# Splitting two scaling steps of a chunked scan between VectorE and ScalarE, and pinning its transposes behind output products

## The chip, the cores and the metric

The kernel runs on one core of a Trainium2 chip. Its engines work side by side, each through its own instructions in order: TensorE (PE in the profile; PEld is its loading of weights), VectorE (DVE), ScalarE (ACT), GpSimd (POOL) and SyncE (SP), whose queue issues the DMA transfers. The metric is device time in microseconds, the median of several runs. All arrays are float32.

## What is computed

One layer over 1024 latent tokens of width 1024, with 256 context tokens ahead. The mixer makes one projection u, splits its columns among a scan, a Fourier mixing and a pooling, and joins the three through w_out. Then comes a feed-forward part with a convolution. Cut to the mixer:

```python
def ssd_chunked(X, dA, B, C, init_state):     # chunks of 128 tokens
    ...
    y_diag = jnp.einsum("bclhn,bcshn,bhcls,bcshp->bclhp", C, B, Lmat, X)
    ...
    y_off = jnp.einsum("bclhn,bchpn,bhcl->bclhp", C, states, jnp.exp(A_cs))
    return (y_diag + y_off).reshape(b, L, h, p), final_state

def ssd_gate_norm(y, xs, z, d_skip, norm_w):
    bsz, L = z.shape[:2]
    y = (y + xs.astype(jnp.float32) * d_skip.astype(jnp.float32)[:, None]).reshape(bsz, L, SSD_WIDTH)
    y = (y * jax.nn.silu(z.astype(jnp.float32))).reshape(bsz, L, SSD_GROUPS, SSD_WIDTH // SSD_GROUPS)
    y = (y * lax.rsqrt(jnp.mean(y * y, -1, keepdims=True) + EPS)).reshape(bsz, L, SSD_WIDTH)
    return (y * norm_w).astype(z.dtype)

def token_mixer(...):
    xs, bm, cm, dt, dA = ssd_prep(u, ...)
    y, s_f, s_b = ssd_bidir(xs, bm, cm, dt, dA, init_f, init_b)
    y_ssd = ssd_gate_norm(y, xs, u[..., OFF_Z:OFF_XBC], d_skip, norm_w)
    y_fnet = fourier_mix(u[..., OFF_FNET:OFF_POOL], fnet_w)
    y_pool = pool_mix(u[..., OFF_POOL:N_IN], pool_w, pool_scale)
    return jnp.concatenate([y_ssd, y_fnet, y_pool], axis=-1) @ w_out, s_f, s_b
```

## The kernel before, in words

The scan has 8 heads of 64 columns in 2 groups, and runs over 8 chunks of 128 tokens in both directions (d = 0, 1). The change touches the stretch from about 240 to 400 us, between the input projection and the second pair of output tiles.

**States.** state_step(n, d) makes one step of the recurrence: xw on POOL (L685), two products on PE into pst (L710), the old state times its decay on DVE (128x512, L712), plus pst (L715), and a store to s_scratch on SP (L717). The steps are issued between the products of the Fourier and pooling projections. four_weights loads cf (two DMAs, L732 and L733) and multiplies it on PE into pPQ (L738).

**Chunk outputs.** chunk_load brings M (the local products), S (the states) and z (the gate) of a chunk. chunk_y starts y on POOL (L900), makes the products po with the states (two, one for each group) and pd with M on PE (L908, L912), scales po by the decay ecs into t1 on DVE (two instructions of 128x512, one for each group, L914), adds pd (L918) and the two directions of t1 (L920), multiplies by z (L921), and sums the squares on ScalarE (L924 to L928: Square with a sum, Ln, Exp). chunk_norm refines the inverse root by a newton step on 128x2 numbers (sv at L933, then L146, L147, L148 and L150) and multiplies y by it (L935). chunk_out transposes y on PE into pyt (L940), and ScalarE writes yT (L944). Y(i) issues the norm of the chunk before, the y of chunk order[i], and the transposes of the chunk before; the order is 4, 5, 6, 7, 3, 2, 1, 0. There is one buffer of t1 and two each of y, M, S and z.

**Pooling.** pool_mix subtracts the inputs from the pooled sums and mends the edges on DVE (L860, L863, L864), then multiplies on PE into ppool (L871).

**Output products.** out_tiles((7, 6), todo) sums the output tiles pout7 and pout6 over eight slices k of 128 of the 1024 joined columns, in the order KO = 0, 1, 2, 3, 4, 6, 5, 7 (L1010). Each float32 factor is held as a high and a low part (L218 and L219: woh and wol of the weights, yh and yl of the inputs), and three of the four products are summed. wo_prep(i) loads slice KO[i] of w_out into one of two raw buffers (wor, L974), multiplies it by the gate's row g1b (L975; g1b is loaded in wo_prep(0), L971), and splits it: the multiplication on POOL for odd i and on DVE for even i, the low part on the other of the two. fp_split and y_split do the same for the Fourier, pooled and scanned inputs. todo[i] is issued ahead of the products of the i-th slice:

```python
    todo = {
        0: [lambda: fp_split(0, 2, 1), lambda: wo_prep(5), lambda: pool_mix(1, p1), lambda: wo_prep(6), lambda: fp_split(3), lambda: wo_prep(7)],
        1: [Y(5)],
        3: [Y(6)],
        4: [Y(7)],
        7: [Y(8)],
    }
    out_tiles((7, 6), todo)
```

The code gives the instructions in program order; a scheduler then sets each engine's order, so work that is ready early can move ahead of its place in the code.

## Time and profile before

| | us |
|---|---|
| median of 3 runs (1203.28 to 1203.91) | 1203.84 |
| the profiled execution | 1204.77 |
| its span | 1202.9 |
| PE busy in it | 1129.9 (94%) |
| DVE busy | 984.6 (82%) |
| POOL busy | 609.5 (51%) |
| ACT busy | 461.1 (38%) |

The granted clock of PE is 0.981 of its full speed over the whole span. The busy shares are means over stages that differ, so the stretch of the change is read by itself. In the rows below, times are microseconds from the start of the span unless marked ns. A timeline row gives start, duration, engine, line, operation, out<-in, shape and count, and in brackets the idle time of the engine just before with what ended it. Chunk and buffer numbers are left out of names: y is the y of any chunk.

### The profile page before, as it was taken

The page shows a single profiled execution, that of the slowest core. Times are in us where ns is not written, and L with a number is a line of the kernel's source. Part 1 is how long each engine was busy: PE and PEld are TensorE (multiplying, and loading weights), DVE is VectorE, ACT ScalarE, POOL GpSimd, SP SyncE. Part 2 cuts the span into 40 slices and gives each one's busy share as a digit, 9 for nine tenths or more (in the row PEclk, how much of TensorE's full clock was granted, in tenths as well). Part 3 has the DMA queues.
Part 4 walks back from the last instruction along what each step waited for, and adds up shares of the span by engine and source line. Part 5 has one row for each costly group of instructions (what it writes and reads, how often), then busy time and mean ns, then how long its engine had stood idle before and what let it go on. Part 6 is the DMA issues. An engine that isn't in the chain of part 4 may idle for free.

```text
span 1202.9 us, 15202 instructions
## 1 busy us (share of the span) xinstructions
PE 1129.9 (94%) x5328; PEld 918.1 (76%) x5328; DVE 984.6 (82%) x1395; ACT 461.1 (38%) x790; POOL 609.5 (51%) x482
## 2 busy tenths in 40 slices
PE   4999999989878999899999999999999999999986
PEld 1698887777756787788888787888888888888864
DVE  4788787688899789799999968787777877777966
ACT  1273566721344232433232343333333334343553
POOL 0010122244254025664556477767676767676756
PEclk9999999999999999899999999999999999999988
DMA  9849465567524404223555346665556555555513
GB/s 309 283 163 324 128 213 167 170 195 221 189 89 166 148 35 141 97 88 108 172 166 176 118 154 219 192 199 175 182 183 190 193 192 190 188 184 184 197 40 140
DMA packets 151875, 206.48 MB, mean 172 GB/s; under 512 B 12253, under 2 KB 89067, under 8 KB 151799
## 3 DMA queue, kind: packets, MB, share of 16 engines
q1 hardware_dynamic: 151799, 205.51, 52.7%
q8 instruction: 42, 0.69, 0.2%
q14 instruction: 34, 0.28, 0.1%
HBM read 148.76 MB, written 56.71 MB: 171 GB/s over the span
## 4 chain that ended last, share of the span: by engine, by line
PE 69%; DVE 16%; DMA 6%; issue 3%; ACT 3%; POOL 2%; SPq 0%; DVEq 0%; ACTq 0%; POOLq 0%
PE pu L1353 22%; PE pdn L1187 16%; PE pu L1527 9%; PE pout L1010 4%; PE px L445 4%; PE pz L344 4%; PE pl L1584 3%; PE p L1353 3%; DMA bc<-cs_scratch 2%; DVE cv L1234 1%; PE pu L1245 1%; POOL cv L1224 1%; DMA xr<-in_x_dram 1%; DMA zb_r<-in_w_in_dram 1%; PE pm L298 1%
## 5 line engine op out<-in xcount | busy, mean ns | idle before, releaser
L1234 DVE SCALAR_TENSOR_TENSOR cv<-pu,ffc,cv 128x945 f32<-128x945 f32 (+6 forms) x362 | 425.6, 1180 | 74.1 <-ACT cv L1212 64.3
L1187 PE MATMUL pdn<-wd,gh 128*128 128x512 f32 x576 | 180.7, 395 | 0.3 <-DVE xt L1190 0.3
L1187 PEld LDWEIGHTS pdn<-wd,gh 128*128 128x128 f32 x576 | 108.2, 188 | 25.8 <-DVE xt L1190 1.0
L1187 PE MATMUL pdn<-wd,gl 128*128 128x512 f32 x288 | 113.6, 394 | 0.0
L1190 DVE TENSOR_TENSOR xt<-xt,pdn 128x512 f32<-128x512 f32 x128 | 87.4, 683 | 28.8 <-PE pdn L1187 24.4
L219 POOL TENSOR_TENSOR wul<-wur,wuh 128x1024 fp32r<-128x1024 f32 x29 | 72.3, 2495 | 39.3 <-ACT wuh L218 30.7
L1455 POOL TENSOR_TENSOR wdr<-wdr,g2b 128x512 f32<-128x512 f32 x44 | 57.4, 1309 | 54.7 <-DMA wdr<-in_ffn_w_down_dram 53.1
L219 POOL TENSOR_TENSOR S<-wur,S 128x384 fp32r<-128x384 f32 (+2 forms) x75 | 62.6, 861 | 36.8 <-ACT S L218 24.4
L1481 POOL TENSOR_TENSOR cv<-cv,cv 128x512 f32<-128x512 f32 x44 | 57.9, 1336 | 27.7 <-ACT cv L1480 27.7
L1212 ACT ACTIVATE cv<-pu,ffc 128x1024 f32<-128x1024 f32 (+3 forms) x46 | 53.4, 1164 | 43.5 <-PE pu L1353 21.5
L1353 PE MATMUL pu<-T,S 128*128 128x512 f32 x270 | 67.5, 393 | 0.4 <-POOL S L219 0.4
L644 POOL TENSOR_TENSOR bc<-bc,ncs 128x256 f32<-128x256 f32 x32 | 25.7, 807 | 76.4 <-DMA bc<-cs_scratch 62.1
L1187 PEld LDWEIGHTS pdn<-wd,gl 128*128 128x128 f32 x288 | 54.1, 188 | 12.8
L1480 ACT ACTIVATE cv<-cv 128x512 f32<-128x512 f32 x44 | 25.5, 625 | 90.9 <-DVE cv L1234 90.9
L1353 PEld LDWEIGHTS pu<-T,S 128*128 128x128 f32 x270 | 50.5, 188 | 12.8 <-POOL S L219 0.8
L1353 PE MATMUL pu<-h2h,wuh 128*128 128x512 f32 x150 | 59.1, 394 | 0.0
L206 POOL TENSOR_TENSOR h2l<-h2t,h2h 128x512 fp32r<-128x512 f32 x14 | 20.5, 1475 | 75.9 <-DVE h2h L205 75.9
L1353 PE MATMUL pu<-h2h,wul 128*128 128x512 f32 x150 | 59.0, 393 | 0.0
L1353 PE MATMUL pu<-h2l,wuh 128*128 128x512 f32 x150 | 58.5, 390 | 0.0
L219 POOL TENSOR_TENSOR gl<-cv,gh 128x512 fp32r<-128x512 f32 x44 | 56.7, 1309 | 1.5 <-PE pl L1584 0.7
L219 POOL TENSOR_TENSOR wd<-wdr,wd 128x512 fp32r<-128x512 f32 x42 | 53.8, 1303 | 4.7 <-ACT wd L218 4.6
L1527 PE MATMUL pu<-h2h,wuh 128*128 128x512 f32 x176 | 55.3, 395 | 0.0
(407 smaller groups left out, 2939.6 us busy)
## 6 DMA issues: line engine op xcount, KB each, us to landing
xt<-x_scratch SPq DMA_DIRECT2D x144, 256.0 KB
x_scratch<-xt SPq DMA_DIRECT2D x144, 256.0 KB
wur<-in_ffn_w_up_dram SPq DMA_DIRECT2D x44, 512.0 KB
wad<-in_w_ada_dram SPq DMA_DIRECT2D x32, 512.0 KB
wdr<-in_ffn_w_down_dram SPq DMA_DIRECT2D x44, 256.0 KB
wa<-in_w_ada_dram SPq DMA_DIRECT2D x32, 256.0 KB
bc<-cs_scratch SPq DMA_DIRECT2D x32, 256.0 KB
xr<-in_x_dram SPq DMA_DIRECT2D x8, 512.0 KB
```

The lines of the kernel that those rows point to most:

```text
L219: return (eng or G).tensor_tensor(lo, raw, hi.bitcast(F32), op=ALU.subtract)
L344: TE.matmul(pt[:, j * 512 : j * 512 + ZW], a, b[:, k % 4, :], start=first and i == 0, stop=last and i == 2)
L445: TE.matmul(pt[:, q * 512 : q * 512 + 512], a[:, k, :], b[q][:, k, :], start=k == 0 and i == 0, stop=k == KD - 1 and i == 2)
L1010: TE.matmul(pt[:, nb * 512 : nb * 512 + 512], u, v[:, nb * 512 : nb * 512 + 512], start=first and i == 0, stop=last and i == 2)
L1187: TE.matmul(pt, u_, wd[nb][:, v_, :], start=i == 0, stop=i == n - 1)
L1190: V.tensor_tensor(xt, xt, pt, op=ALU.add)
L1212: tap[0] = S.activation(acc[:, a * 64 : b * 64], pt[:, a * 64 : b * 64], AF.Identity, bias=ffc[:, 396 + ct : 397 + ct], scale=factor(0, 0))
L1234: last = V.scalar_tensor_tensor(dst, pv[:, r0 + dy : r1 + dy, c0 + dx : c1 + dx], factor(dy, dx), dst, op0=ALU.mult, op1=ALU.add)
L1353: TE.matmul(dst, a[k][u], b[k][w], start=start and k == 0 and j == 0, stop=k == n - 1 and j == 2, skip_group_check=True)
L1455: G.tensor_tensor(raw, raw, g2b[:, s], op=ALU.mult)
L1481: G.tensor_tensor(acc[:, s], acc[:, s], acc_v[:, s], op=ALU.mult)
L1527: TE.matmul(pt[:, q * 512 : q * 512 + 512], a[:, k, :], b[q][:, k, :], start=k == 0 and j == 0, stop=k == KD - 1 and j == 2)
```

## The change

The state's decay product is cut in two: DVE keeps group 0 (128x256), ScalarE does group 1 in four pieces of 128x64, one for each head. In the same way DVE keeps t1's group 0, and ScalarE does group 1 in eight pieces of 128x64. chunk_norm makes two newton steps on 128x1 numbers, one for each group, each of three instructions with a scalar by pointer, and two products of 128x256. Y is split for the chunks in out_tiles: Ya issues the norm, the next chunk's y and load; Yb issues the transposes two or one slices later, and behind() pins them on their engines after the last output product that was issued. pool_mix(1) is pinned in the same way at slice 3 instead of standing at slice 0, and wo_prep(6), wo_prep(7) and fp_split(3) move with it. The first pair of output tiles is followed by the last transposes.

```diff
--- before.py
+++ after.py
@@ -709,9 +709,11 @@
         for g in range(2):
             TE.matmul(pt[:, g * 256 : g * 256 + 256], btok[g][:, ch, :], xw[:, g, :], start=True, stop=True)
         dst, src = qt(stag[d](), f"st{d}_{n + 1}", [P, 2, 256]), state[d]
-        V.tensor_tensor(dst[:].rearrange("p g (h q) -> p g h q", q=64),
-                                      src[:].rearrange("p g (h q) -> p g h q", q=64),
-                                      dv(etot, ch, d).unsqueeze(3).broadcast_to([P, 2, 4, 64]), op=ALU.mult)
+        V.tensor_tensor(dst[:, 0].rearrange("p (h q) -> p h q", q=64), src[:, 0].rearrange("p (h q) -> p h q", q=64),
+                        dv(etot, ch, d)[:, 0].unsqueeze(2).broadcast_to([P, 4, 64]), op=ALU.mult)
+        for h in range(4):
+            S.activation(dst[:, 1, h * 64 : h * 64 + 64], src[:, 1, h * 64 : h * 64 + 64], AF.Identity,
+                         scale=etot[:, ch, 8 + 4 * d + h : 9 + 4 * d + h])
         V.tensor_tensor(dst, dst, pt[:].rearrange("p (g n) -> p g n", g=2), op=ALU.add)
         state[d] = dst
         nc.sync.dma_start(ss[ch + 1 - 2 * d][:, d, :], dst[:].rearrange("p g n -> p (g n)"))
@@ -910,10 +912,11 @@
         pd = psb(f"pd{ch}")
         for i in range(8):
             TE.matmul(pd[:, i * 64 : i * 64 + 64], M[:, i, :], xt[:, i * 64 : i * 64 + 64], start=True, stop=True)
-        for g in range(2):
-            V.tensor_tensor(t1[:, g].rearrange("p d (h q) -> p (d h) q", q=64),
-                            pos[g][:].rearrange("p (a q) -> p a q", q=64),
-                            ecs[:, ch, g * 8 : g * 8 + 8].unsqueeze(2).broadcast_to([P, 8, 64]), op=ALU.mult)
+        V.tensor_tensor(t1[:, 0].rearrange("p d (h q) -> p (d h) q", q=64), pos[0][:].rearrange("p (a q) -> p a q", q=64),
+                        ecs[:, ch, 0:8].unsqueeze(2).broadcast_to([P, 8, 64]), op=ALU.mult)
+        for a in range(8):
+            S.activation(t1[:, 1, a // 4, (a % 4) * 64 : (a % 4) * 64 + 64], pos[1][:, a * 64 : a * 64 + 64], AF.Identity,
+                         scale=ecs[:, ch, 8 + a : 9 + a])
         yv = y[:].rearrange("p (g n) -> p g n", g=2)
         V.tensor_tensor(y, y, pd, op=ALU.add)
         for d in range(2):
@@ -931,8 +934,9 @@
     def chunk_norm(ch, y, yv, ssq, r):
         v = sm.tile([P, 2], F32, tag="sv", name=f"sv{ch}")
         V.tensor_scalar(v, ssq, 1.0 / 256.0, EPS, op0=ALU.mult, op1=ALU.add)
-        r = newton(r, v, 2, f"ssn{ch}")
-        V.tensor_tensor(yv, yv, r.unsqueeze(2).broadcast_to([P, 2, 256]), op=ALU.mult)
+        for g in range(2):
+            q = newton(r[:, g : g + 1], v[:, g : g + 1], 1, f"ssn{ch}{g}")
+            V.tensor_scalar(yv[:, g], yv[:, g], q, None, op0=ALU.mult)
 
     def chunk_out(ch, y, *_):
         py = psb(f"pyt{ch}")
@@ -943,6 +947,21 @@
         for k in range(4):
             S.activation(yT[ch // 2][:, k, (ch % 2) * P : (ch % 2) * P + P], py[:, k * P : k * P + P], AF.Identity,
                          scale=col[:, 48 + k : 49 + k])
+
+    held = [None]
+
+    def Ya(i):
+        def f():
+            chunk_norm(*lastc[0])
+            held[0] = lastc[0]
+            if i < NT:
+                lastc[0] = chunk_y(order[i])
+            if i + 2 < NT:
+                chunk_load(order[i + 2])
+        return f
+
+    def Yb():
+        behind(chunk_out, *held[0])
 
     def Y(i):
 
@@ -1007,8 +1026,15 @@
         b = yl[q][:, k, (t % 4) * P : (t % 4 + 1) * P]
         for i, (u, v) in enumerate(((a, wo[k][0]), (a, wo[k][1]), (b, wo[k][0]))):
             for nb in range(2):
-                TE.matmul(pt[:, nb * 512 : nb * 512 + 512], u, v[:, nb * 512 : nb * 512 + 512],
-                          start=first and i == 0, stop=last and i == 2)
+                lastmm[0] = TE.matmul(pt[:, nb * 512 : nb * 512 + 512], u, v[:, nb * 512 : nb * 512 + 512],
+                                      start=first and i == 0, stop=last and i == 2)
+
+    lastmm = [None]
+
+    def behind(f, *args):
+
+        with tc.issue_after(lastmm[0].ins):
+            f(*args)
 
     def out_tiles(ts, mids={}):
         pts = [psa(f"pout{t}") for t in ts]
@@ -1055,13 +1081,16 @@
     wo_prep(4)
 
     todo = {
-        0: [lambda: fp_split(0, 2, 1), lambda: wo_prep(5), lambda: pool_mix(1, p1), lambda: wo_prep(6), lambda: fp_split(3), lambda: wo_prep(7)],
-        1: [Y(5)],
-        3: [Y(6)],
-        4: [Y(7)],
-        7: [Y(8)],
+        0: [lambda: fp_split(0, 2, 1), lambda: wo_prep(5)],
+        1: [Ya(5)],
+        2: [Yb],
+        3: [lambda: behind(pool_mix, 1, p1), lambda: wo_prep(6), lambda: fp_split(3), lambda: wo_prep(7), Ya(6)],
+        4: [Yb, Ya(7)],
+        6: [Yb],
+        7: [Ya(8)],
     }
     out_tiles((7, 6), todo)
+    Yb()
     slx.close()
     post = ctx.enter_context(tc.tile_pool(name="post", bufs=1, reuse_waits="tile"))
     lng = qt("EM1", "ln1g")
```

The line numbers shift by two to nineteen: L717 becomes L719, L732 L734, L871 L873, L884 L886, L888 L890, L908 L910, L912 L914, L940 L944, L975 L994, L1010 L1029.

The order on the engines at three places. SP's queue around the loads of cf (the Fourier weights), in the middle of the state scan; st0_2 is the state of direction 0 after two steps. Before:

```order
L884 DMA M5_2657<-m_scratch 128x1024
L717 DMA s_scratch<-st0_2_2519 128x512
L732 DMA cf_2587<-in_k_c64_dram 128x256
L717 DMA s_scratch<-st1_2_2528 128x512
L733 DMA cf_2587<-in_fnet_w_dram 128x2x64
L888 DMA z4_2655<-z_scratch 128x512
L650 DMA m_scratch<-EU01_2551 128x512
```

and changed:

```order
L719 DMA s_scratch<-st1_1_2463 128x512
L886 DMA M5_2697<-m_scratch 128x1024
L993 DMA wor0_3176<-in_w_out_dram 128x1024
L734 DMA cf_2611<-in_k_c64_dram 128x256
L735 DMA cf_2611<-in_fnet_w_dram 128x2x64
L719 DMA s_scratch<-st0_2_2527 128x512
L719 DMA s_scratch<-st1_2_2540 128x512
```

The loads of cf now stand ahead of both stores of step 2 and behind the load of wor0; the load of z4 is behind both stores. Further down the load of g1b stands behind the store of st0_7 instead of behind that of st1_6.

PE from the first products of slice 3 on, around ppool10 and ppool11, the pooled products. Before:

```order
L1010 MATMUL pout7_3238<-woh3_3211,yh1_3202 128x512 x2
L1010 MATMUL pout6_3239<-woh3_3211,yh1_3202 128x512 x2
L871 MATMUL ppool10_3269<-pT1_3049,PQW_2585 128x512
L871 MATMUL ppool11_3270<-pT1_3049,PQW_2585 128x512
L908 MATMUL po20_3317<-S2_3045,cT6_1341 128x256 x2
L908 MATMUL po21_3320<-S2_3045,cT7_1540 128x256 x2
L912 MATMUL pd2_3323<-xt1_1854,M2_3043 128x64 x8
L940 MATMUL pyt3_3344<-ident_75,y3_3111 128x128 x4
L1010 MATMUL pout7_3238<-wol3_3212,yh1_3202 128x512
L908 MATMUL po10_3396<-S1_3152,cT6_1341 128x256 x2
L908 MATMUL po11_3399<-S1_3152,cT7_1540 128x256 x2
L912 MATMUL pd1_3402<-xt0_1853,M1_3150 128x64 x8
```

and changed:

```order
L1029 MATMUL pout6_3350<-woh2_3307,yh1_3313 128x512 x2
L1029 MATMUL pout6_3350<-wol2_3308,yh1_3313 128x512
L944 MATMUL pyt3_3451<-ident_75,y3_3215 128x128 x2
L1029 MATMUL pout6_3350<-wol2_3308,yh1_3313 128x512
L1029 MATMUL pout6_3350<-woh2_3307,yl1_3314 128x512 x2
L944 MATMUL pyt3_3451<-ident_75,y3_3215 128x128 x2
L1029 MATMUL pout7_3349<-woh3_3322,yh1_3313 128x512 x2
L1029 MATMUL pout6_3350<-woh3_3322,yh1_3313 128x512 x2
L873 MATMUL ppool10_3483<-pT1_3148,PQW_2609 128x512
L873 MATMUL ppool11_3484<-pT1_3148,PQW_2609 128x512
L910 MATMUL po10_3524<-S1_3263,cT6_1341 128x256 x2
L910 MATMUL po11_3527<-S1_3263,cT7_1540 128x256 x2
```

po2, pd2 (chunk 2) and pyt3 (the transposes of chunk 3) stood behind the pooled products. Now pyt3 stands among the last products of slice 2, behind the first four of them, and po2 and pd2 stand ahead of the products of slice 1. Behind the pooled products follow po1 and pd1 at once.

DVE ahead of the last edge of the pooled inputs (L864, now L866), for which ppool10 waits. Before:

```order
L860 SCALAR_TENSOR_TENSOR pT1_3049<-s8_1_3189,pe_1064,pT1_3049 64x1008
L863 TENSOR_TENSOR s8_1_3189<-s8_1_3189,pe_1064 64x8 x2
L860 SCALAR_TENSOR_TENSOR pT1_3049<-s16_1_3191,pe_1064,pT1_3049 64x1008
L864 TENSOR_TENSOR pT1_3049<-s8_1_3189,pT1_3049 64x8 x2
L863 TENSOR_TENSOR s16_1_3191<-s16_1_3191,pe_1064 64x8 x2
L933 TENSOR_SCALAR sv3_3305<-ss3_3135 128x2
L864 TENSOR_TENSOR pT1_3049<-s16_1_3191,pT1_3049 64x8 x2
L146 TENSOR_TENSOR ssn3_t_3307<-sr3_3138 128x2
```

and changed:

```order
L939 TENSOR_SCALAR y3_3215<-y3_3215,ssn30_q_3387 128x256
L144 TENSOR_SCALAR ssn31_q_3393<-ssn31_t_3390,sr3_3249 128x1
L923 TENSOR_TENSOR y2_3396<-y2_3396,t1_2_3398 128x512
L939 TENSOR_SCALAR y3_3215<-y3_3215,ssn31_q_3393 128x256
L924 TENSOR_TENSOR y2_3396<-y2_3396,z2_3146 128x512
L862 SCALAR_TENSOR_TENSOR pT1_3148<-s8_1_3300,pe_1064,pT1_3148 64x1008
L865 TENSOR_TENSOR s8_1_3300<-s8_1_3300,pe_1064 64x8 x2
L862 SCALAR_TENSOR_TENSOR pT1_3148<-s16_1_3302,pe_1064,pT1_3148 64x1008
L866 TENSOR_TENSOR pT1_3148<-s8_1_3300,pT1_3148 64x8 x2
L865 TENSOR_TENSOR s16_1_3302<-s16_1_3302,pe_1064 64x8 x2
L994 TENSOR_TENSOR wor5_3489<-wor5_3489,g1b_3174 128x1024
L866 TENSOR_TENSOR pT1_3148<-s16_1_3302,pT1_3148 64x8 x2
```

Chunk 3's norm and the y of chunk 2 (up to the product with z2) stood behind the last edge; now they stand ahead of it, and so does the product of wor5 with g1b.

## Rows read from the trace of the kernel before

**Rows 1.** Busy time by stretch: PE, PEld, DVE, ACT, POOL (instructions), clock, DMA, GB/s.

```profile
240.00:400.00 160.00, 136.25 (x652) 111.00 (x651) 142.51 (x241) 50.74 (x128) 66.70 (x43) 0.95 0.55 175
400.00:440.00 40.00, 40.00 (x174) 32.13 (x173) 29.55 (x80) 6.75 (x14) 0.00 (x0) 1.00 0.23 85
```

**Rows 2.** What PE waited for, 238 to 400 us: total, times, longest.

```profile
PE pPQ L738 <- DMA cf<-in_fnet_w_dram: 2.5, 1, 2.5
```

**Rows 3.** Timeline of PE, 359 to 396 us: start, duration, line, names, idle before.

```profile
359.49 3.64 PE L871 MATMUL ppool<-pT,PQW 128*128 128x512 f32 x4 [3.81 <-DVE pT L864]
...
376.18 0.73 PE L1010 MATMUL pout<-woh,yh 128*128 128x512 f32 x2 [0.97 <-ACT woh L218]
377.69 0.73 PE L1010 MATMUL pout<-wol,yh 128*128 128x512 f32 x2 [0.77 <-DVE wol L219]
...
380.17 0.63 PE L940 MATMUL pyt<-ident,y 128*128 128x128 f32 x4
...
387.29 1.09 PE L940 MATMUL pyt<-ident,y 128*128 128x128 f32 x4 [3.03 <-DVE y L935]
...
394.95 0.73 PE L1010 MATMUL pout<-woh,yh 128*128 128x512 f32 x2
```

**Rows 4.** What DVE waited for, 286 to 360 us: total, times, longest.

```profile
DVE sv L933 <- ACT z L924: 2.0, 2, 1.0
DVE y L918 <- PE pd L912: 1.1, 1, 1.1
DVE t L914 <- PE po L908: 1.0, 2, 0.9
DVE ssn_t L146 <- ACT sr L928: 0.6, 1, 0.6
```

**Rows 5.** Chain of waits, 235 to 450 us: chunk 2's products on PE.

```profile
363.12 1.73 PE po L908 x8
364.85 1.75 PE pd L912 x16
```

**Rows 6.** Timeline of DVE, 289 to 392 and 456 us.

```profile
289.42 1.23 DVE L975 TENSOR_TENSOR wor<-wor,g1b 128x1024 f32<-128x1024 f32 x1 [3.40 <-DMA g1b<-ada_scratch]
...
299.46 0.15 DVE L146 TENSOR_TENSOR ssn_t<-sr 128x2 f32<-128x2 f32 x1
...
302.84 2.32 DVE L150 TENSOR_TENSOR ssn_q<-sr,ssn_t 128x2 f32<-128x2 f32 x1
...
321.67 2.33 DVE L146 TENSOR_TENSOR ssn_t<-sr 128x2 f32<-128x2 f32 x1 [0.64 <-ACT sr L928]
...
333.37 1.87 DVE L147 TENSOR_TENSOR ssn_t<-ssn_t,sv 128x2 f32<-128x2 f32 x1
...
359.27 0.24 DVE L864 TENSOR_TENSOR pT<-s,pT 64x8 f32<-64x8 f32 x2
...
363.16 1.23 DVE L219 TENSOR_TENSOR wol<-wor,woh 128x1024 fp32r<-128x1024 f32 x1 [1.00 <-PE ppool L871]
...
384.35 2.80 DVE L935 TENSOR_TENSOR y<-y,ssn_q 128x512 f32<-128x512 f32 x1
...
388.86 1.21 DVE L219 TENSOR_TENSOR wol<-wor,woh 128x1024 fp32r<-128x1024 f32 x1
...
456.02 0.27 DVE L141 TENSOR_SCALAR ln_t<-ln_r,ln_v 128x1 f32<-128x1 f32 x1
```

**Rows 7.** Timeline of POOL beside two of those DVE instructions.

```profile
321.62 2.36 POOL L219 TENSOR_TENSOR wol<-wor,woh 128x1024 fp32r<-128x1024 f32 x1 [5.11 <-ACT woh L218]
...
455.69 1.57 POOL L206 TENSOR_TENSOR h2l<-h2t,h2h 128x512 fp32r<-128x512 f32 x1 [1.54 <-DVE h2h L205]
```

**Rows 8.** Instructions grouped by line and shape, 238 to 400 us: busy, mean ns, idle.

```profile
L712 DVE TENSOR_TENSOR st<-st,etot 128x512 f32<-128x512 f32 x14 | 12.2, 882 | 0.1
...
L914 DVE TENSOR_TENSOR t<-po,ecs 128x512 f32<-128x512 f32 x16 | 10.5, 682 | 1.1 <-PE po L908 1.0
...
L944 ACT ACTIVATE yT<-pyt,col 128x128 f32<-128x128 f32 x31 | 9.1, 367 | 22.8 <-PE pyt L940 22.8
```

## The prediction

> **What bounds the kernel now.** I read four views in this order. First the busy time by stretch [rows 1]: from 240 to 400 us, where all code of the change runs, PE is busy 136.25 of 160 us, DVE 142.51 and ScalarE only 50.74. In the next 40 us PE has no idle time at all. So what the change can win at most is PE's 23.75 idle us in that stretch, plus what is run there at the lower clock (granted share 0.95). Behind 400 us PE works through the same products in the same order, so I carry whatever shift stands at the start of pout5, the first product of the second pair of output tiles, unchanged to the end.
>
> Second, what PE waits for [rows 2, 3]: normed chunks before a transpose (3.03 us at 387.29), the last pooled edge before ppool10 (3.81 us at 359.49), the Fourier weights (2.5 us), and one wait each for the high and the low part of a weight of the output product (0.97 and 0.77). Nearly all of these releasers are DVE work. Third, what DVE waits for from 286 to 360 us [rows 4]: 2.0 + 1.1 + 1.0 + 0.6 = 4.7 us, so it is nearly saturated, and its last row before ppool10 [359.27 in rows 6] is what PE waits for.
>
> Fourth, DVE's and POOL's instructions beside each other [rows 6, 7]. A small DVE product of 128x2 numbers takes 0.15 us at 299.46 and 2.33 us at 321.67, while POOL works on wol from 321.62 for 2.36 us: DVE stands until POOL is through. The same shows at 302.84 and 333.37 and, for a 128x512 product, at 384.35 (2.80 us). A TENSOR_SCALAR on 128x1 ran 0.27 us at 456.02 inside a POOL instruction of 1.57 us, so that form did not stand.
>
> **The change part by part.** The chain that I cost is DVE from the load of g1b (the gate's row that scales the weights of the output product; DVE waits 3.40 us for it at 289.42 [rows 6]) to the last L864 row, then PE from ppool10 to pout5.
>
> Step 1, SP's queue. The loads of cf stand ahead of the two stores of step 2 of the scan, so they no longer wait for st1_2, and PE's 2.5 us at pPQ [rows 2] should go. The load of g1b is moved behind one more store (st0_7), but everything that feeds it starts earlier. I take −2.5; bounds 0 (the stores set g1b's load as before) and −3.4 (DVE's whole wait for it).
>
> Step 2, the state steps. DVE loses half of 14 products of 0.88 us [rows 8], 14 x 0.44 = 6.2 us; ScalarE gets 56 pieces of 128x64. No such piece is in this trace. The nearest row, 31 pieces of 128x128, is 9.1 us busy, 0.29 each; half as many columns give 0.15 to 0.29, so four take 0.6 to 1.2 us where DVE's whole product took 0.88. Bounds on the path: −6.2, if all the freed vector time counted, to 14 x (1.2 − 0.88) = +4.5. I take 0: PE's projections lie over these steps and PE's idle time there is small; without that cover the upper end counts.
>
> Step 3, waits of DVE. With t1's second half on ScalarE and the norms issued later, the 4.7 us of waits [rows 4] can fill with other work. I take −3.0 (0 to −4.7): the wait for y's sum of squares is a round trip through ScalarE and stays where nothing else is ready.
>
> Step 4, DVE's work up to the last L864. Five second halves of t1 and the first half of chunk 4's, which now runs ahead of g1b, go: 6 x 0.68 [rows 8] = −4.1. Against this the order puts five products of chunk 2 ahead (5 x 0.68 = +3.4), chunk 3's norm (some six small ones of 0.15 and two half products that together come to 0.68: +1.6), the product of wor5 (1.23 as at 289.42, +1.2) and, for chunks 4 to 7, two more small ones each (4 x 0.3 = +1.2). Sum +3.3.
>
> Step 5, the norm's small products become 128x1 TENSOR_SCALARs. Three of the old kind stood 2.32, 2.33 and 1.87 us instead of 0.15 [rows 6], 6.1 us lost. If the new form never stands, as at 456.02, all goes; if the multiply of y behind it catches the same POOL instruction instead, nothing. I take half, −3.1.
>
> These five give −2.5 + 0 − 3.0 + 3.3 − 3.1 = −5.3: ppool10 would start at 359.49 − 5.3 = 354.2.
>
> Step 6, PE behind ppool10. po2 and pd2 (1.73 and 1.75 us [rows 5]) and chunk 3's transposes (some 0.35 of the 0.63 at 380.17, since its end lies beside the next product) are already done: −3.8.
>
> Step 7, the waits behind ppool10. Before, they are 0.97, 0.77 and 3.03, and the transposes behind the last take 1.09 instead of 0.63, so some 0.5 more is lost: 5.3 us that the pinned order could remove. But the last weights come serially: with two raw buffers the load of wor6 waits for wol3, that of wor7 for wol6. Before, wol3 starts at 363.16 and wol7 ends at 388.86 + 1.21 = 390.07, 26.9 us later; PE starts pout5 4.9 us after that. From the end of ppool10 (363.13) to pout5 (394.95 [rows 3]) it is 31.8 us, of which 31.8 − 5.3 − 3.8 = 22.7 is work that remains. So PE would reach wol7 before it is there unless that chain shortens. I take 3.1 us back for a new wait on woh7 and wol7, net −2.2 (bounds: −5.3, chain in time, and +3.8, chain as slow as before, which eats step 6 as well).
>
> The sum is −5.3 − 3.8 − 2.2 = **−11.3 us** against the profiled execution's 1204.77, so 1193.5. The median of the runs is 0.93 lower; the forecast against it is **1192.5 us**.
>
> The pins add waits on PE: pyt3, ppool10, pyt2, pyt1 and pyt0 stand behind whole groups of output products. Behind each of them PE's own queue waits, the next chunk's po and the output products; ScalarE's yT waits in turn. I cost the pins at nothing beyond steps 6 and 7, since the products placed ahead of them are the cover; the price without it is in the rivals.
>
> **A rule that speaks against it.** The row for ScalarE [rows 8] says 0.29 us for a piece of 128x128, and step 4 takes DVE's 0.68 off and counts ScalarE's pieces at nothing: DVE's first half of t1 and the addition of pd, 1.36 us, run meanwhile. Eight pieces at 0.15 to 0.29 take 1.2 to 2.3 us, so they just fit or miss by up to 0.9. The Trainium skill, ScalarE: Activation LUTs, section Rules for kernel authors, says to put plain multiplications on VectorE and not on ScalarE. By the same page's section What ACT_TABLE_LOAD costs, an estimate for eight such pieces with one operand by pointer is 2.0 us; by that, 2.0 less 1.36 stays uncovered, 0.6 us a chunk or 4.8 in eight, and the sum would be 1197.3 instead of 1192.5. No run here yet shows such a piece. The rule's mechanism, with a price from rows, is rival (b).
>
> **The rivals.** (a) Slower. The norms of chunks 3 to 0 run where POOL prepares the last weights. If each catches a POOL instruction as y1's did, a small product loses 2.32 − 0.15 = 2.2 and the multiply 2.80 − 0.68 = 2.1 [rows 6], 4.3 us a chunk, and with the transposes pinned PE can't pass them: 4 x 4.3 = +17.2, so 1192.5 + 17.2 = 1209.7. It decides from 11.3 / 4 = 2.8 us a chunk. For it: 384.35. Against it: the new small form at 456.02, and that before pays part of this already.
>
> (b) ScalarE's latency lies on each chunk's path: the middle of 1.2 to 2.3 is 1.8, less 0.68 is 1.1, times 8 chunks +8.8: 1201.3. That is about no change. For it: DVE adds both halves of t1 at once, so it needs the last piece. Against it: ScalarE is idle two thirds of the stretch [rows 1].
>
> (c) What is freed ahead of ppool10 is eaten by what was placed ahead of it (steps 1 to 5 sum to 0); steps 6 and 7 alone give −6.0: 1197.8. For it: chunk 2 and chunk 3's norm on DVE are as long as what was removed.
>
> (d) The waits go as meant: step 3 −4.7, step 5 −6.1, step 7 −5.3, the others as above: −2.5 − 4.7 + 3.3 − 6.1 − 3.8 − 5.3 = −19.1, so 1184.7. Against it: the serial chain of weights.
>
> **How the numbers follow.** Forecast with its near neighbours (1188 to 1196) 0.50, (c) 0.18, (d) 0.12, (b) 0.11, (a) 0.09. A measurement here can tell about 0.2%, 2.4 us, so "the same" is 1201.4 to 1206.2. Faster are the forecast, (c), (d) and a third of (b): 0.84; the same 0.07; slower 0.09. The range runs from 1183, below (d), to 1202, above (b)'s middle; outside lie (a), half of (b) and some of (d), 0.18 together. Step 2's ends (1186.3 and 1197.0) and step 7's upper end (1198.5) lie inside.
>
> **What would show it.** Right: no wait at pPQ; DVE's load of g1b some 2.5 us earlier; ppool10 near 354 and pout5 near 384; the norm's small products at 0.3 us beside busy POOL; a wait of a few us for woh7 or wol7 where pout7 ends its sum. Steps 2 and 4 are wrong if DVE waits for ScalarE's pieces at L923 (adding t1) or at the state's addition L717 by more than 0.5 us each. The forecast is wrong if PE's waits at pyt3 and ppool10 together grow by more than 11 us over the 3.8 at ppool10 alone, or if the products behind 400 us don't keep the shift.

## The result

The changed kernel took 1196.26 us (median of 4 runs, 1194.45 to 1197.75) against 1203.88 of the kernel before: a ratio of 0.9937, 95% interval 0.992 to 0.9954. It is faster by 7.6 us, some two thirds of the 11.3 that were forecast. Run again beside three experiments, it came to 1197.46 against 1201.95, 4.5 us faster, 0.9954 (0.9937 to 0.9971). Its profiled execution took 1194.45, the fastest of its first four, with a span of 1192.7.

The span is shorter by 10.2 us, but not all of it belongs to the change. The first product of the states' start, pinit, stands ahead of all changed work. First before, then after (timelines of PE: start, duration, line, names):

```profile
238.82 1.89 PE L698 MATMUL pinit<-xwc,btc 128*128 128x256 f32 x8
```

```profile
236.18 1.89 PE L698 MATMUL pinit<-xwc,btc 128*128 128x256 f32 x8
```

2.6 us were gone by then. In a second execution of the kernel before (u_pins, below) the same product started at 235.74, so this part is scatter. I therefore measure from pinit on. The kernel before started pout5, the first product of the second pair of output tiles, 394.95 − 238.82 = 156.1 us behind it, in the second execution 155.6. The changed kernel did so after 387.06 − 236.18 = 150.9, in its own second execution 151.7. So the changed stretch gave **4.6 us** (means of two), nearer to the second measurement than to the first. It also holds a little more: the last four transposes, 0.36 us, stand behind the start of pout5 in the kernel before and ahead of it in the changed one. Behind pout5 the profiled execution is another 2.3 us shorter, 805.6 to the span's end against 808.0. I take that for scatter too: the second executions have 808.1 (changed) and 810.4 (before), and the other ten traces of this document lie between 806.8 and 808.0.

### The profile page after: what moved, and what is told of

It reads as the page before. It is cut to its first block, busy times and chain, and to the rows that moved or that the text cites. A ratio compares the mean times of both kernels' runs of the same rounds, so it can differ in the third digit from the quotient of the medians.

```text
span 1192.7 us, 15375 instructions
## 1 busy us (share of the span) xinstructions
PE 1124.2 (94%) x5328; PEld 913.3 (77%) x5328; DVE 974.3 (82%) x1411; ACT 488.1 (41%) x910; POOL 607.9 (51%) x482
## 4 chain that ended last, share of the span: by engine, by line
PE 57%; DVE 13%; issue 3%; POOL 3%; ACT 1%; DMA 1%; SPq 0%; DVEq 0%; ACTq 0%; POOLq 0%
PE pu L1382 21%; PE pdn L1216 15%; PE pu L1556 9%; PE pout L1029 4%; PE pl L1613 3%; PE p L1382 2%; DVE cv L1263 1%; PE pu L1274 1%; DVE y L923 1%; POOL cv L1253 1%; DVE xa L1109 1%; DVE xa L1110 1%; DMA wur<-in_ffn_w_up_dram 0%; DVE h2h L205 0%; DVE y L939 0%
## 5 line engine op out<-in xcount | busy, mean ns | idle before, releaser
L219 POOL TENSOR_TENSOR S<-wur,S 128x384 fp32r<-128x384 f32 (+2 forms) x75 | 62.6, 860 | 36.8 <-ACT S L218 23.7
L1241 ACT ACTIVATE cv<-pu,ffc 128x1024 f32<-128x1024 f32 (+3 forms) x46 | 53.4, 1163 | 42.3 <-PE pu L1382 21.5
L644 POOL TENSOR_TENSOR bc<-bc,ncs 128x256 f32<-128x256 f32 x32 | 23.3, 732 | 80.7 <-DMA bc<-cs_scratch 66.2
```

Source lines behind the costliest of these rows:

```text
L219: return (eng or G).tensor_tensor(lo, raw, hi.bitcast(F32), op=ALU.subtract)
L1241: tap[0] = S.activation(acc[:, a * 64 : b * 64], pt[:, a * 64 : b * 64], AF.Identity, bias=ffc[:, 396 + ct : 397 + ct], scale=factor(0, 0))
```

## The profile after

Busy time by stretch, the answer to [rows 1]:

```profile
240.00:400.00 160.00, 139.53 (x675) 113.38 (x674) 138.58 (x282) 80.25 (x252) 65.73 (x42) 0.95 0.56 186
400.00:440.00 40.00, 40.00 (x190) 32.48 (x189) 28.62 (x68) 10.78 (x22) 3.62 (x3) 1.00 0.10 40
```

PE's idle time from 240 to 400 fell from 23.75 to 20.47 us and ScalarE took up 29.5 us more; DVE is at 138.58. What PE waited for, against [rows 2, 3] (us in total, times, longest):

```profile
PE pyt L944 <- DVE ssn_q L144: 5.1, 2, 2.7
PE ppool L873 <- DVE pT L866: 4.8, 1, 4.8
PE pout L1029 <- ACT woh L218: 4.2, 1, 4.2
...
PE pPQ L740 <- DMA cf<-in_fnet_w_dram: 0.9, 1, 0.9
```

The wait for the Fourier weights fell from 2.5 to 0.9. The wait at ppool10 is 4.8 instead of 3.81, and 4.2 us for woh7, the high part of the last weights, are new. PE's timeline shows where:

```profile
354.28 3.75 PE L873 MATMUL ppool<-pT,PQW 128*128 128x512 f32 x4 [4.76 <-DVE pT L866]
...
380.91 1.22 PE L1029 MATMUL pout<-woh,yh 128*128 128x512 f32 x2 [4.19 <-ACT woh L218]
382.55 1.22 PE L1029 MATMUL pout<-wol,yh 128*128 128x512 f32 x2 [0.42 <-DVE wol L219]
...
387.06 0.72 PE L1029 MATMUL pout<-woh,yh 128*128 128x512 f32 x2
```

ppool10 starts at 354.28 (forecast: 354.2) and pout5 at 387.06 (forecast: 383.7). That ppool10 meets its forecast is luck: of the 5.2 us by which it comes earlier, 2.6 were gone at pinit. From pinit on it comes 2.2 us earlier (118.1 against 120.4, means of two), where the sum had 5.3. The products behind the wait take 1.22 us a pair, where they took 0.73 in [rows 3].

ScalarE's pieces and the new norm, grouped by line and shape (busy, mean ns, idle before):

```profile
L715 ACT ACTIVATE st<-st,etot 128x64 f32<-128x64 f32 x56 | 15.0, 336 | 11.2 <-DVE st L717 10.2 <-DMA s_scratch<-st 0.7 <-DMA m_scratch<-EU 0.2
L918 ACT ACTIVATE t<-po,ecs 128x64 f32<-128x64 f32 x64 | 14.3, 331 | 15.9 <-PE po L910 9.8 <-DVE y L923 6.1
...
L939 DVE TENSOR_SCALAR y<-y,ssn_q 128x256 f32<-128x256 f32 x16 | 8.0, 533 | 0.0
...
L141 DVE TENSOR_SCALAR ssn_t<-sr,sv 128x1 f32<-128x1 f32 x16 | 3.7, 265 | 0.9 <-ACT sr L931 0.8
```

## Where each kernel loses or gains

The distances in this table are differences of starts in each kernel's timelines, of one execution each, from the first pinit to the product of wor0 with g1b, to ppool10, and to pout5; the last column is the ratio to the kernel before of the runs on the same chip.

| kernel | wor0 | ppool10 | pout5 | ratio (95% interval) |
|---|---|---|---|---|
| before | 50.6 | 120.7 | 156.1 | 1 |
| before again (u_pins) | 51.6 | 120.0 | 155.6 | 1.0008 (0.9992 to 1.0023) |
| changed | 49.0 | 118.1 | 150.9 | 0.9937 (0.992 to 0.9954) |
| changed again (after2) | 48.5 | 118.1 | 151.7 | 0.9954 (0.9937 to 0.9971) |
| u_state: states on VectorE | 51.8 | 122.6 | 155.2 | 0.9969 (0.9954 to 0.9983) |
| u_t1: t1 on VectorE | 49.6 | 123.8 | 155.2 | 0.9954 (0.9939 to 0.997) |
| u_norm: old norm | 49.3 | 117.5 | 147.9 | 0.993 (0.9912 to 0.9949) |
| u_pins2: old order | 49.0 | 113.3 | 149.1 | 0.9928 (0.9907 to 0.995) |
| u_pool: pooled products at slice 0 | 48.7 | 111.4 | 146.8 | 0.9937 (0.9915 to 0.996) |
| o_pins: new order alone | 52.1 | 127.9 | 159.4 | 1.0011 (0.9996 to 1.0027) |
| shares: ScalarE's two shares alone | 48.6 | 112.1 | 147.9 | 0.9935 (0.9916 to 0.9953) |
| raw7: changed, third raw buffer | 44.9 | 114.9 | 142.3 | 0.9914 (0.9891 to 0.9938) |
| norm_raw7: raw7 with the old norm | 48.1 | 117.1 | 148.0 | 0.9935 (0.9913 to 0.9956) |
| shares_raw7: shares and the buffer | 48.6 | 112.2 | 148.9 | 0.9946 (0.9927 to 0.9966) |

The distances of one kernel repeat within about 1 us where they could be compared; raw7's first one is an exception told below. The intervals of the ratios are some 0.4% wide, so the ratios alone tell few of the variants apart, and I use the two columns together.

## The experiments

My theory was that of the prediction: vector time ahead of ppool10 sets the pace, and behind it the serial chain of the last weights. The rivals were that the pins bring the gain, or that ScalarE's latency eats it.

**The states' share undone (u_state).**

```diff
-        V.tensor_tensor(dst[:, 0]..., src[:, 0]..., dv(etot, ch, d)[:, 0]...)
-        for h in range(4):
-            S.activation(dst[:, 1, h * 64 : h * 64 + 64], ..., scale=etot[...])
+        V.tensor_tensor(dst[:]..., src[:]..., dv(etot, ch, d)..., op=ALU.mult)
```

> The changed kernel with the state's decay product whole on VectorE again (14 products of 128x512). My theory (step 2 priced at nothing): the freed vector time lies beside the projections, so the time stays within 2 us of the changed kernel's 1196.3, and pooled product ppool10 stays near 354. Rival 1: the freed 6.2 us of vector time count, so the time goes back by some 4 to 6 us, to 1200 to 1202, and ppool10 to about 358. Rival 2: ScalarE's four pieces lengthen each step, so undoing them makes it 1 to 4 us faster, 1192 to 1195.

Measured: 1199.47 us, 0.9969. ppool10 came 122.6 us behind pinit instead of 118.1 and pout5 at 155.2 instead of 151.3. My price of nothing fell and the first rival holds, at 4 us in the trace (by the ratios, 0.9969 against the changed kernel's 0.9937 and 0.9954, it is 2 to 4). Three of these are there at wor0 already, and PE's list of waits says where they begin:

```profile
PE pPQ L738 <- DMA cf<-in_fnet_w_dram: 3.5, 1, 3.5
```

3.5 us for cf, with SP's queue in the order of before again, st0_2 and st1_2 among the loads of cf (written out: st0_2, cf, st1_2, cf). So it was the states' share that moved the loads of cf ahead, not another part of the change: with the shares alone (shares) they also stand ahead of both stores. The queue is not the whole of it, though: pPQ itself starts 25.4 us behind pinit here and 24.1 and 23.7 in the changed kernel, some 1.5 of the 3 us. The rest comes between pPQ and the load of g1b, and no run parts the later steps of the queue from the vector time that is freed there.

**t1's share undone (u_t1).**

```diff
-        V.tensor_tensor(t1[:, 0]..., pos[0]..., ecs[:, ch, 0:8]..., op=ALU.mult)
-        for a in range(8):
-            S.activation(t1[:, 1, a // 4, ...], pos[1][:, a * 64 : a * 64 + 64], ..., scale=ecs[...])
+        for g in range(2):
+            V.tensor_tensor(t1[:, g]..., pos[g]..., ecs[:, ch, g * 8 : g * 8 + 8]..., op=ALU.mult)
```

> The changed kernel with both halves of t1 on VectorE again. My theory: eight second halves of 0.68 us, of which six stand ahead of the last pooled edge, count in full there: some 3 to 4 us slower than 1196.3, about 1200, with ppool10 near 358. Rival (ScalarE's latency on each chunk's path, 1.7 us where VectorE took 0.68): the same or up to 4 us faster, 1192 to 1196.

Measured: 1196.96 us, 0.9954, so the runs can't tell it from the changed kernel; the 1200 of the theory was not reached, and by time alone the rival's "the same" would stand. The trace can tell them apart: from wor0 to ppool10 it takes 361.47 − 287.27 = 74.2 us instead of 69.1 and 69.6, 4.8 more, and PE waits longest there:

```profile
361.47 3.73 PE L873 MATMUL ppool<-pT,PQW 128*128 128x512 f32 x4 [6.08 <-DVE pT L866]
```

That is what the theory gave (4.1 from six halves). From ppool10 on it gives 1.8 back (392.81 − 361.47 = 31.3 instead of 33.1), since the last weights are ready by then: its list has no wait for woh7. The rival, ScalarE's latency, would have made this kernel faster ahead of ppool10; it falls.

**The norm undone (u_norm).**

```diff
-        for g in range(2):
-            q = newton(r[:, g : g + 1], v[:, g : g + 1], 1, f"ssn{ch}{g}")
-            V.tensor_scalar(yv[:, g], yv[:, g], q, None, op0=ALU.mult)
+        r = newton(r, v, 2, f"ssn{ch}")
+        V.tensor_tensor(yv, yv, r.unsqueeze(2).broadcast_to([P, 2, 256]), op=ALU.mult)
```

> The changed kernel with one newton step on 128x2 numbers and one multiply of 128x512 for a chunk again. My theory (step 5): the 128x2 products stand until POOL is through, some 3 us in sum: 1199 to 1200, with small products of over 1 us in the timeline. Rival: the multiply of y catches the same POOL instruction either way, so within 1 us of 1196.3.

Measured: 1193.61 us, 0.993, and a pout5 that comes 3.4 us earlier than in the changed kernel's two executions. The new norm isn't worth 3 us; if anything it costs. The rival's 1 us is missed too, by the median, though the interval (0.9912 to 0.9949) reaches it. One chunk's norm in the changed kernel, DVE and then POOL:

```profile
312.22 0.46 DVE L141 TENSOR_SCALAR ssn_t<-sr,sv 128x1 f32<-128x1 f32 x2 [0.40 <-ACT sr L931]
312.59 0.27 DVE L142 TENSOR_SCALAR ssn_t<-ssn_t 128x1 f32<-128x1 f32 x2
312.78 0.33 DVE L144 TENSOR_SCALAR ssn_q<-ssn_t,sr 128x1 f32<-128x1 f32 x2
313.03 2.72 DVE L939 TENSOR_SCALAR y<-y,ssn_q 128x256 f32<-128x256 f32 x2
```

```profile
313.21 2.39 POOL L219 TENSOR_TENSOR wol<-wor,woh 128x1024 fp32r<-128x1024 f32 x1 [4.71 <-ACT woh L218]
```

and the same chunk with the old norm:

```profile
311.94 0.16 DVE L150 TENSOR_TENSOR ssn_q<-sr,ssn_t 128x2 f32<-128x2 f32 x1
312.14 0.69 DVE L938 TENSOR_TENSOR y<-y,ssn_q 128x512 f32<-128x512 f32 x1
```

```profile
312.34 2.71 POOL L219 TENSOR_TENSOR wol<-wor,woh 128x1024 fp32r<-128x1024 f32 x1 [6.11 <-PE po L910]
```

The three pairs on 128x1 show what they take with POOL idle. Both multiplies begin some 0.2 us ahead of POOL's wol. The undivided one is through in 0.69 us, and it is POOL that takes longer (2.71). The two halves take 2.72 us together: the first 0.35, and the second, which begins at 313.29 beside the running wol, 2.46. It ends 0.16 us behind POOL, so it waited POOL out. Only 0.6 of the 3.4 us are there at ppool10 (117.5 against 118.1). The rest comes behind it: with the old norm chunk 0's squares are through before wor7 is, and woh7 starts at 376.61 right behind wor7's end at 376.58, where in the changed kernel it starts 2.0 us behind it (see raw7).

**The order undone: a repeat, and then the experiment (u_pins, u_pins2).**

> The changed kernel with the order of before in the output products (no pins, pool_mix at slice 0, all of the last weights prepared at slice 0), ScalarE's shares and the norm as changed. My theory: po2 and pd2 go back behind ppool10 (3.8 us) but ppool10 comes some 4 to 5 us earlier, since chunk 2's y and chunk 3's norm no longer stand ahead of it, and the weights are ready sooner: about the changed kernel's time, 1194 to 1198. Rival 1: the pins are what pays: 1200 or more. Rival 2: the pins cost what PE waits at pyt3 (2.3) and for woh7 (4.2): 1190 to 1193.

By a slip in its edit this kernel was the kernel before itself, letter for letter, so that expectation was put to no test. It serves as a second execution of before: 1203.4 us, 1.0008. The experiment proper:

```diff
-        0: [lambda: fp_split(0, 2, 1), lambda: wo_prep(5)],
-        1: [Ya(5)],
-        2: [Yb],
-        3: [lambda: behind(pool_mix, 1, p1), lambda: wo_prep(6), lambda: fp_split(3), lambda: wo_prep(7), Ya(6)],
-        4: [Yb, Ya(7)],
-        6: [Yb],
-        7: [Ya(8)],
+        0: [lambda: fp_split(0, 2, 1), lambda: wo_prep(5), lambda: pool_mix(1, p1), lambda: wo_prep(6), lambda: fp_split(3), lambda: wo_prep(7)],
+        1: [Y(5)],
+        3: [Y(6)],
+        4: [Y(7)],
+        7: [Y(8)],
```

> The changed kernel with the order of before in the output products (Y in place of Ya and Yb, pool_mix and the last weights at slice 0), ScalarE's shares and the two newton steps as changed. My theory: po2, pd2 go back behind ppool10 and the norm of chunk 1 waits on POOL again (about 7 us back), but ppool10 comes 4 to 5 us earlier, since chunk 2's y and chunk 3's norm no longer stand ahead of it: 2 to 4 us slower than the changed kernel, ratio 0.995 to 0.998. Rival 1: the pins are all that pays, ratio 0.999 to 1.002. Rival 2: the pins cost what PE waits for woh7, ratio 0.988 to 0.992.

Measured: 1193.81 us against the changed kernel's 1197.46 on the same chip, 0.9928. That is nearest to the second rival, whose range ended at 0.992. The first rival falls: with the shares, the pins bring nothing. ppool10 comes 4.8 us earlier, as I had it:

```profile
349.32 3.78 PE L873 MATMUL ppool<-pT,PQW 128*128 128x512 f32 x4 [4.88 <-DVE pT L866]
...
369.24 0.69 PE L944 MATMUL pyt<-ident,y 128*128 128x128 f32 x2 [2.14 <-DVE y L939]
...
383.25 0.63 PE L944 MATMUL pyt<-ident,y 128*128 128x128 f32 x4 [1.62 <-DVE y L939]
```

Behind it 35.8 us follow to pout5 (383.25, the last transposes, and three pairs of products of pout6 lie ahead of that), 2.7 more than with the pins. I had expected 7 to come back, and so a slower kernel.

**The new order alone (o_pins).** The kernel before with Ya, Yb, behind() and the new todo; nothing else.

> The kernel before with the new order of the output products alone (Ya, Yb, the pins, pool_mix at slice 3); state steps, t1 and norm as before. My theory: the vector work ahead of ppool10 is longer by 4.1 (t1) and some 3 (stalled norms), and PE waits for cf longer, so some 5 us of the gain go: ratio 0.997 to 1.000. Rival 1: the pins are all that pays, ratio 0.992 to 0.995. Rival 2: without the shares the pinned transposes wait longer and it ends slower than before, above 1.002.

Measured: 1203.36 us, 1.0011 (0.9996 to 1.0027): no gain, just above what the theory gave, and the first rival falls. The second, above 1.002, lies within the interval, and its longer waits are in the trace. Its pout5 comes 3.5 us later than before (159.4 against 155.9).

```profile
356.64 1.09 PE L940 MATMUL pyt<-ident,y 128*128 128x128 f32 x4 [3.86 <-DVE y L935]
362.54 3.46 PE L871 MATMUL ppool<-pT,PQW 128*128 128x512 f32 x4 [4.81 <-DVE pT L864]
...
386.12 1.08 PE L940 MATMUL pyt<-ident,y 128*128 128x128 f32 x4 [4.92 <-DVE y L935]
```

Three of the five pinned steps wait for vector work: pyt3 3.86, ppool10 4.81, pyt1 4.92 us; pyt2 and pyt0 don't.

**The pooled products unpinned (u_pool).** The changed kernel with pool_mix, wo_prep(6), fp_split(3) and wo_prep(7) at slice 0 again and without a pin; the transposes stay pinned.

> The changed kernel with pool_mix, wo_prep(6), fp_split(3) and wo_prep(7) back at slice 0 and not pinned, while the transposes stay pinned (Ya, Yb). If it is the pooled products' place behind chunk 2's y and chunk 3's norm that costs: ppool10 some 4 to 5 us earlier and the last weights earlier, ratio 0.988 to 0.992. If it is the pinned transposes that cost: 0.994 to 0.996, as the changed kernel.

Measured: 1193.49 us, 0.9937. The trace speaks for the first case: ppool10 at 111.4, 6.7 us earlier than in the changed kernel, and pout5 at 146.8, 4.5 earlier. The ratio lies between the two cases, with both in its interval, so the runs don't settle it.

**A third buffer for the last weights (raw7).**

```diff
-        raw = ring("raw", f"wor{k}")
+        raw = qt("q2", f"wor{k}") if i == 7 else ring("raw", f"wor{k}")
```

> The changed kernel with a third raw buffer for the last slice of w_out, so that its load no longer waits for the low part of slice 6; POOL's product wor7 then stands ahead of the split of the scanned input, and woh7 ahead of chunk 0's squares. My theory (step 7, the serial chain of weights): the wait of 4.2 us for woh7 and the 2 to 3 us of lower clock behind it go, pout5 starts near 381, 4 to 7 us faster than the changed kernel, ratio 0.988 to 0.990. Rival: another wait ends last there (y1's norm for pyt1, or the split of the scanned input), and less than 2 us come of it.

Measured: 1193.4 us, 0.9914 (0.9891 to 0.9938), 4.1 us below the changed kernel on the same chip and the lowest ratio of all, though just above the 0.988 to 0.990 expected. The rival, under 2 us, falls by the trace: from ppool10 to pout5 it takes 379.21 − 351.77 = 27.4 us instead of 32.8 and 33.5.

```profile
351.77 3.75 PE L873 MATMUL ppool<-pT,PQW 128*128 128x512 f32 x4 [4.76 <-DVE pT L866]
...
379.21 0.74 PE L1029 MATMUL pout<-woh,yh 128*128 128x512 f32 x2
```

The mechanism shows in three engines. The changed kernel, POOL, DVE and then ScalarE:

```profile
372.64 2.38 POOL L219 TENSOR_TENSOR yl<-yT,yh 128x1024 fp32r<-128x1024 f32 x1 [4.94 <-ACT yh L218]
375.00 2.82 POOL L994 TENSOR_TENSOR wor<-wor,g1b 128x1024 f32<-128x1024 f32 x1
```

```profile
371.90 3.68 DVE L923 TENSOR_TENSOR y<-y,t 128x512 f32<-128x512 f32 x2
375.62 2.75 DVE L924 TENSOR_TENSOR y<-y,z 128x512 f32<-128x512 f32 x1
```

```profile
378.44 0.42 ACT L927 ACTIVATE z<-y 128x256 f32<-128x256 f32 x1 [5.88 <-POOL wor L994]
...
379.82 1.04 ACT L218 ACTIVATE woh<-wor 128x1024 fp32r<-128x1024 f32 x1
```

POOL splits the scanned input ahead of the product of wor7; that ends at 377.82; and ScalarE's woh7 then stands behind the squares of chunk 0, which wait for DVE. DVE in turn stood behind POOL: its second product of the first row took 2.90 us and the next one 2.75, where such a product takes 0.69. So woh7 starts 2.0 us behind wor7's end. With the third buffer:

```profile
366.83 2.93 POOL L994 TENSOR_TENSOR wor<-wor,g1b 128x1024 f32<-128x1024 f32 x1 [1.62 <-DMA wor<-in_w_out_dram]
370.16 2.38 POOL L219 TENSOR_TENSOR yl<-yT,yh 128x1024 fp32r<-128x1024 f32 x1 [0.40 <-ACT yh L218]
```

```profile
369.91 1.11 ACT L218 ACTIVATE woh<-wor 128x1024 fp32r<-128x1024 f32 x1
```

wor7 is multiplied first and woh7 made at 369.91. And the clock, in the stretch right behind the place where the changed kernel had waited, and the same stretch of raw7 (columns as in [rows 1], the clock third from the end):

```profile
382.00:386.00 4.00, 3.58 (x9) 2.77 (x9) 1.80 (x3) 0.00 (x0) 0.00 (x0) 0.50 0.64 253
```

```profile
378.00:382.00 4.00, 4.00 (x20) 3.01 (x19) 3.90 (x8) 2.49 (x6) 0.00 (x0) 1.00 0.97 381
382.00:386.00 4.00, 3.12 (x15) 2.25 (x14) 3.36 (x11) 1.20 (x2) 0.00 (x0) 1.00 0.74 268
```

0.50, the lower of its two levels (1.2 GHz), against 1.00. The profiled raw7 was also 4 us quicker from pinit to wor0, where its instructions stand in the order of the changed kernel, and it is the fastest of its six runs; its distance of 142.3 is flattered by that, the 27.4 is not.

**Do the gains add? (norm_raw7, shares, shares_raw7.)**

> The changed kernel with the norm of before (one newton step on 128x2, one multiply of 128x512) and the third raw buffer for the last slice. If the two gains add (some 2 to 3 us of vector time ahead of ppool10, some 4 to 5 us of waiting for woh7): ratio 0.986 to 0.990. If the earlier vector work only runs into the same serial chain: as with the buffer alone, 0.990 to 0.993.

> The kernel before with ScalarE's two shares alone: state steps and t1 as changed, norm and order of the output products as before. By the theory that the shares carry the gain and that pins and two-step norm cost: ratio 0.988 to 0.993, ppool10 about 113 us behind the first product of the states' start. By the rival that shares, norm and pins need each other: 0.996 to 1.000.

> The kernel before with ScalarE's two shares and the third raw buffer. In the order without pins PE waits behind ppool10 for chunks' norms, not for woh7, so the buffer should bring under 1 us over the shares alone: ratio 0.987 to 0.993. The rival, that the last weights come late in any order, gives 3 us or more: 0.984 to 0.989.

Measured: 1193.78 (0.9935), 1194.23 (0.9935) and 1195.92 us (0.9946). They don't add. With the old norm the buffer leaves 30.9 us from ppool10 to pout5, where u_norm had 30.5: in place of woh7 PE waits for a chunk's norm. Of the 7.1 us of such waits in the whole stretch 3.1 lie behind ppool10.

```profile
PE pyt L943 <- DVE y L938: 7.1, 4, 3.1
```

The shares alone gave a ratio just above the expected range and the distance to ppool10 that I had named (112.1 for 113). The buffer brings them nothing, as expected, since there PE waits for norms already, behind ppool10 4.8 us of the 5.9 without the buffer and 4.2 of the 7.4 with it (the ratio is again above the range that I gave):

```profile
PE pyt L943 <- DVE y L938: 5.9, 4, 3.2
```

```profile
PE pyt L943 <- DVE y L938: 7.4, 4, 3.3
```

So ScalarE's two shares, without new norm and new order, gave what the whole change gave.

**The changed kernel again (after2).**

> The changed kernel once more, so that it stands beside the other three on one chip. Expected: 0.992 to 0.995 of the kernel before, ppool10 near 354 and pout5 near 387, a wait for woh7 of about 4 us.

Measured: 1197.46 us, 0.9954, just above what was expected, ppool10 at 353.79, pout5 at 387.32, a wait of 3.9 us for woh7.

## Why the prediction was right, and where its steps were not

The sign and the time were right, 1196.3 against 1192.5 in a range of 1183 to 1202, but the sum held only in part. It had −11.3 us; the runs gave −7.6 and −4.5 and the changed stretch −4.6. That the time lies in the range owes something to the range's width, and rival (c)'s 1197.8 lies nearer to it than the forecast.

- **Step 1** (−2.5 to wor0): measured 48.5 and 49.0 against 50.6 and 51.6 from pinit, −2.4 in the mean. The size was right, the reason only in part. PE's wait for cf did shrink, but pPQ starts only 1.3 us earlier from pinit, and the second load of cf was not issued earlier: 257.99 − 236.18 = 21.8 us behind pinit against 260.27 − 238.82 = 21.5. The rest comes behind pPQ. u_state shows that the states' share brings it, which step 2 had at nothing; that attribution was wrong.
- **Step 2** (0) was mis-sized: undoing it cost about 4 us, three at wor0, which are step 1's gain. The pieces themselves were priced well: 15.0 us for 56, 0.27 each, four in 1.07 of the 0.6 to 1.2 estimated, and DVE waited only 0.4 us for them. So the sign that was named for a wrong step 2, over 0.5 us of such a wait, stayed away, and the step was wrong on the other side.
- **Steps 3, 4 and 5** (together −2.8 from wor0 to ppool10): measured 69.1 and 69.6 against 70.1 and 68.5, nothing. Step 4 held in both halves: t1's share is worth 4.8 (4.1 in the sum), and the order that puts chunk 2's y, chunk 3's norm and wor5 ahead of ppool10 costs 4.8 to 6.7 (u_pins2, u_pool; 3.4 + 1.6 + 1.2 = 6.2 in the sum). **Step 5 failed**: −3.1 was taken as half of the stalls, and the row at 313.03 shows the lower bound that the prediction named, the multiply that catches the same POOL instruction instead. Step 3's waits went from 4.7 to some 3, not by 3.
- **Step 6** (−3.8): po2, pd2 and pyt3 are done ahead of ppool10, as the order shows. But that only led PE to the next wait sooner.
- **Step 7** (−2.2) was mis-sized, and somewhat over half of the gap is here. Steps 6 and 7 were to give −6.0; from 35.5 to 33.1 they gave −2.4, which is 3.6 of the 6.7 us that the stretch fell short. The new wait was foreseen, at 3.1 us, a figure taken from no row; it was 4.2 for woh7 and 0.4 for wol7, and six pairs of products ran from 380.91 to 386.70, 5.8 us, where raw7 runs a pair in 0.46, so with the lower clock it came to about 7. I had taken the raw buffers' chain alone; what stood ahead of its links on POOL (the split of the scanned input) and on ScalarE (chunk 0's squares, late because DVE stood behind POOL) I had not costed.

Of the rivals, (a) fell for the whole change but is near to what the new order does alone (o_pins: +3.5 in the stretch, with waits for norms and for the last pooled edge). (b) fell. Eight pieces took 1.75 us,

```profile
360.35 1.75 ACT L918 ACTIVATE t<-po,ecs 128x64 f32<-128x64 f32 x8 [0.94 <-PE po L910]
```

in the middle of the 1.2 to 2.3 estimated, and undoing t1's share made the way to ppool10 longer. The estimate from the Trainium skill (ScalarE: Activation LUTs, What ACT_TABLE_LOAD costs) was 2.0 us for the eight, a little more than measured. The 1197.3 that went with it lies near the measured time, but not for its reason: DVE's list of waits from 285 to 358 us names none for these pieces. The Trainium skill's rule to keep multiplications on VectorE (ScalarE: Activation LUTs, Rules for kernel authors) didn't decide here, where DVE was busy 142.51 of 160 us and ScalarE 50.74. (c) was right on what lies between wor0 and ppool10, nothing, but not on step 1's −2.4 nor on the −6.0 behind ppool10, so that its time came close is luck. (d) is what raw7 came near to behind ppool10, once the chain of weights was cut.

What stays open: whether the pins and the new norm cost time in the runs, as they do in the traces (2.2 to 4.5 us at pout5). The new norm was only undone, never added alone. The intervals of u_norm, u_pins2, u_pool and shares all touch that of the changed kernel. Against the kernel before, only o_pins shows no gain.

## What to carry to other kernels

Work that is freed on a saturated engine pays where the next wait is for that engine; here that was t1 ahead of ppool10, and the states ahead of the load of g1b, in part through the order of the DMA queue. Before a transpose or product is pinned, look at what the pinned place waits for: here the pins only exchanged one idle place for another. A serial chain is costed with what is queued ahead of each of its links on every engine. A third buffer was worth 4.1 us in the changed kernel and nothing in two others, where another wait ended last.

## What the runs showed of the hardware

- TENSOR_SCALAR is no protection against POOL by itself: on 128x1 it ran free beside a POOL instruction (0.27 us at 456.02 in [rows 6]; none of the 38 that start beside one in the changed kernel's trace took longer), on 128x256 the second of two took 2.46 us beside 2.39 us of POOL.
- Who began first decided who waited, in the rows shown: a 128x512 product that began 0.2 us ahead of POOL took 0.69 us, and POOL 2.71 instead of 2.39; two that began while POOL was busy took 2.90 and 2.75.
- A wait of the same length was followed by different times at the lower clock, and once by none. The transposes behind 3.7 us of idle time in the post-norm, and the products that follow, first in the kernel before and then in the changed one:

```profile
483.46 1.12 PE L189 MATMUL h<-ident,xn 128*128 128x128 f32 x4 [3.74 <-ACT h2t L200]
...
488.64 0.63 PE L1245 MATMUL pu<-h2h,wul 128*128 128x512 f32 x1
...
489.34 0.40 PE L1245 MATMUL pu<-h2l,wuh 128*128 128x512 f32 x1
```

```profile
475.02 1.09 PE L189 MATMUL h<-ident,xn 128*128 128x128 f32 x4 [3.69 <-ACT h2t L200]
...
478.05 0.61 PE L1274 MATMUL pu<-h2h,wuh 128*128 128x512 f32 x1
...
478.73 0.40 PE L1274 MATMUL pu<-h2h,wul 128*128 128x512 f32 x1
```

Products of 128x512 took 0.63 us instead of 0.40 until 5.6 us behind the start of the transposes in the kernel before and until 3.4 us in the changed one, at the lower of PE's two levels (granted clock 0.50, 1.2 GHz). In the second executions it is 5.6 and 4.1 us, in nine of the other ten traces 3.0 to 5.6. In the tenth, raw7, the clock didn't fall at all behind the same wait (granted 1.00 from 468 to 472 us):

```profile
468.44 0.66 PE L189 MATMUL h<-ident,xn 128*128 128x128 f32 x4 [3.77 <-ACT h2t L200]
468.85 0.48 PE L1274 MATMUL pu<-h2h,wuh 128*128 128x512 f32 x1
```

The change touches no instruction there, and two kernels with ScalarE's shares (u_pins2, u_pool) have 5.5 and 5.6 as the kernel before has, so this is a part of the scatter of some 3 us between runs of one kernel.
